# Neighbourhood attention stage: V asked for first in each unit, loads of K, Q and the bias tables dealt out one part to a unit

## The chip, the core and the metric

The kernel runs on one core of a Trainium2 chip. The core has a matrix engine (PE, with a separate row PEld for its weight loads), a vector engine (DVE), a scalar engine (ACT), a general engine (POOL) and a queue engine (SP) that only issues DMAs; 16 DMA engines move data between device memory (HBM) and the on-chip memory. Each engine runs its own instructions in their program order. The metric is device time in microseconds (us) of one execution, lower is better.

## The reference

One layer of a hybrid encoder, 1024 tokens of width 1024. After an RMS norm, one projection makes the inputs of two attention groups; their outputs are gated, joined and projected back, and a per-layer embedding is added. The change lies in group B alone, the neighbourhood attention: 8 heads of width 64 on a grid of 16 rows by 64 columns, where a query sees 8 rows by 16 columns of keys.

```python
s = jnp.einsum('bhrcd,bhrikd->bhrcik', qg, kg) * (d ** -0.5) + bias[None]
s = jnp.where(valid[:, None, :], s, NEG)
pr = jax.nn.softmax(s.reshape(B, H, R, GRID_W, kr * GRID_W), axis=-1)
o = jnp.einsum('bhrcik,bhrikd->bhrcd', pr, vg)
yb = neighbourhood_attention(qb, kb, vb, na_rpb[i]) * jax.nn.silu(zb)
```

## The kernel before, in words

All arithmetic is in float32, with operands split in a high and a low part where more precision is needed. The stages follow each other: norm and input projection (to about 304 us), neighbourhood attention (about 304 to 469 us) with the z projection mixed in as filling work, differential attention, output projection, gate.

The neighbourhood stage works through 32 units, numbered here 0 to 31: `(pr, R, j)` with 4 pairs of heads `pr`, 2 halves of the grid rows `R`, 4 column strips `j`. Four units with the same pair and half are called a block here, so a pair has two blocks. In iteration `i` of the loop the engines get, in this order: the loads of `pre(i + 1)`; the transposes `na_t` of unit i-1; the scores' bias and exponential `na_e` of unit i (DVE, ACT); filling matmuls; the gating `na_y` of unit i-2; the scores `na_s` of unit i+1 (PE, tile `nsp`, line 647); filling matmuls; the product with V, `na_pv`, of unit i-1 (PE, tile `npv`, line 700).

The loads come from HBM, where the projection stage had put Q, K and V:

- V: one tile `Vw` for each unit, in three DMAs of 64 or 48 KB, two on SP's queue and one on POOL's. `load_v` asks for it two units ahead of the unit whose loads `pre` handles.
- Q: for each block three parts of 256 KB (`Q1` upper and lower half from `qbh`, `Q2` from `qbl`). The scores of the block's first unit need all three.
- K: for each pair three parts of 512 KB (`kbh`, `kbl`, `kbh` again into `K2`).
- R: for each pair two bias tables of 376 KB, one for each head; `na_e` needs them from the pair's first unit on.
- `zraw`: 512 KB of weights for the z projection, asked for within the filling work, on the same SP queue.

There is no scheduler: the order of instructions on every engine is that of the code. SP's DMAs take eight semaphores in turn, and each issue waits, besides its buffer, for the one that had the same semaphore before, so that at most eight of SP's DMAs are under way.

Of the kernel before, what the change touches and what calls it, by code (L numbers as in the profile page):

```python
# [8 lines left out]
F32R = mybir.dt.float32r  # L9
# [6 lines left out]
P = 128  # L16
D = 1024
S = 1024
# [13 lines left out]
def ap_of(t, off, dims):  # L32
    return bass.AP(tensor=t.tensor, offset=t.offset + off, ap=[list(d) for d in dims])
# [7 lines left out]
def layer_kernel(ctx, tc, x, p, ngr, w_in, w_out, gains, lamv, t5p, rpbp, w_gate, w_ple,  # L41
# [9 lines left out]
    def nm(s):  # L51
        cnt[0] += 1
        return f"{s}_{cnt[0]}"

    def T8(shape, dt=F32, n="t8"):
        return sb.tile(shape, dt, name=nm(n), tag="b8", bufs=16)

    def T4(shape, dt=F32, n="t4"):
        return sb.tile(shape, dt, name=nm(n), tag="b4", bufs=8)

    def TA(shape, dt=F32, n="ta"):
        return sb.tile(shape, dt, name=nm(n), tag="a4", bufs=6)
# [4 lines left out]
    def T15(shape, dt=F32, n="t15"):  # L67
        return sb.tile(shape, dt, name=nm(n), tag="b2", bufs=NB2)
# [24 lines left out]
    def raw(a):  # L93
        return a.bitcast(F32) if a.dtype == F32R else a

    def ld(o, i):
        return nc.sync.dma_start(raw(o), raw(i))  # L97
# [504 lines left out]
    kb = {}  # L602
    qb = {}
    Rt = {}
    Vw = {}

    def load_k(pr):
        k1 = T8([P, 2, S], F32R, n="K1")
        h, l = qkd["kb"]
        for (dst, s) in ((k1[0:64], h), (k1[64:128], l), (K2[pr % 2][0:64], h)):  # L610
            ld(dst, s[pr].rearrange("(h d) s -> d h s", h=2))
        kb[pr] = k1

    def load_q(pr, R):
        q1 = T4([P, 2, 512], F32R, n="Q1")
        h, l = qkd["qb"]
        for (dst, s) in ((q1[0:64], h), (q1[64:128], h), (Q2[R][0:64], l)):
            ld(dst, s[pr, :, R * 512:(R + 1) * 512].rearrange("(h d) s -> d h s", h=2))
        qb[pr, R] = q1

    def load_r(pr):
        r = []
        for h in range(2):
            t = TA([P, 752], n="R")
            ld(t, ap_of(rpbp, (2 * pr + h) * 23 * 48 + 1, [[48, 8], [1, 16], [1, 752]]))
            r.append(t)
        Rt[pr] = r

    def load_v(pr, R, j):
        w = WID[j]  # L630
        v = T15([P, 3, P], n="Vw")
        for m in range(3):
            r0 = 4 * R + 4 * m
            (ld if m < 2 else stp)(v[0:4 * w, m], ap_of(vbd, (r0 * 64 + COL0[j]) * 512 + pr * P, [[64 * 512, 4], [512, w], [1, P]]))
        Vw[pr, R, j] = v
# [85 lines left out]
    K2 = []  # L721
    Q2 = []
# [109 lines left out]
    def pre(i):  # L832
        if i >= len(units):
            return
        pr, R, j = units[i]
        if j == 0:
            if R == 0:
                load_q(pr, 1)
            elif pr + 1 < 4:
                load_q(pr + 1, 0)  # L840
        if (R, j) == (0, 2) and pr + 1 < 4:
            load_k(pr + 1)
        if (R, j) == (1, 1) and pr + 1 < 4:
            load_r(pr + 1)
        if i + 2 < len(units):
            load_v(*units[i + 2])

    LA = 8
    load_p(1)
# [86 lines left out]
    def s7():  # L936
# [11 lines left out]
        30: lambda: u_load(30),  # L948
        31: lambda: u_load(31),
        NS - 7: lambda: (na_consts_k(), load_k(0)),  # L950
        NS - 5: lambda: (load_r0(), x_reload()),
        NS - 4: lambda: (z_load(COL["zb"], True), z_load(COL["zb"] + P, True)),
        NS - 2: lambda: (na_consts_q(), load_q(0, 0), load_v(0, 0, 0), load_v(0, 0, 1), z_split(COL["zb"], 0, 4),
                         z_split(COL["zb"], 4, 8), z_low()),
        NS - 1: lambda: (pre(0), x_resplit()),
        NS: na_consts_k,
    }
    lam_in = []
    normed = []
    for i in range(len(steps) + 2):  # L960
# [8 lines left out]
        if got:  # L969
            n, t0, c = got  # L970
# [314 lines left out]
    for i in range(NU + 3):  # L1285
        if i < NU:
            pre(i + 1)
# [171 lines left out]
```

## Time and profile before

| | |
|---|---|
| time, median of 3 runs | 822.54 us (818.36 to 823.64) |
| the profiled execution's own time | 819.77 us, its span 818.0 us |
| PE busy | 782.3 us, 96% of the span |
| DVE, ACT, POOL busy | 63%, 53%, 35% |
| DMA | 151.99 MB, mean 186 GB/s |

The span runs from the first to the last instruction; the device time has 1.8 us more. A busy share is an average over all stages, and PE counts as busy while its matmuls run at half clock too.

### The profile page before, as it was taken

To read this page: it belongs to the slowest core of one execution; us is meant where nothing else is said; L and a number is where in the kernel's file an instruction comes from. 1 tells how busy PE (TensorE), PEld (TensorE's weight loads), DVE (VectorE), ACT (ScalarE), POOL (GpSimd) and SP (SyncE) were. 2 spreads that over 40 slices of the span, in tenths; PEclk is the share of its full clock that TensorE was granted. 3 is DMA by queue.
4 is the path that set the end of the run, shared out by engine and by line. 5 is a ranking of instruction groups with operands and counts; after the bars stand their busy time and mean duration, and the time that the engine had idled before them with its cause. 6 is when DMAs were issued, how large, how long until landed. Compare 5 with 4: busy or idle time off the path is not lost.

```text
span 818.0 us, 12241 instructions
## 1 busy us (share of the span) xinstructions
PE 782.3 (96%) x4242; PEld 647.7 (79%) x4242; DVE 514.4 (63%) x990; ACT 437.4 (53%) x814; POOL 289.1 (35%) x303
## 2 busy tenths in 40 slices
PE   7999899999989999998989989999999989999997
PEld 6788688888878877776777767888888878888886
DVE  4758985786997675564645577777777652633332
ACT  5865454244545445554545588888898842311120
POOL 1001443261655421231323144777777643100000
PEclk9999899999999999999999999999999999999999
DMA  8855362853788999696967977578576518022322
GB/s 319 323 193 193 117 207 92 306 141 102 196 285 233 220 326 237 151 235 147 213 176 191 256 228 204 135 183 217 161 209 164 194 65 331 29 94 87 97 84 91
DMA packets 116622, 151.99 MB, mean 186 GB/s; under 512 B 25576, under 2 KB 74888, under 8 KB 116432
## 3 DMA queue, kind: packets, MB, share of 16 engines
q1 hardware_dynamic: 111824, 141.46, 59.5%
q0 software_dynamic: 4736, 9.75, 4.1%
q8 instruction: 34, 0.56, 0.3%
q14 instruction: 28, 0.23, 0.1%
HBM read 104.96 MB, written 46.17 MB: 185 GB/s over the span
## 4 chain that ended last, share of the span: by engine, by line
PE 67%; DMA 10%; DVE 9%; ACT 4%; SPq 4%; issue 3%; POOL 1%; DVEq 0%; POOLq 0%; ACTq 0%
PE ips L234 6%; PE ips L236 6%; PE ips L235 6%; PE dsp L1066 6%; DMA Vw<-vb 5%; PE gps L1259 4%; PE gps L1261 4%; PE gps L1260 4%; SPq L97 4%; PE dtp L1108 3%; PE ntp L685 2%; PE pps L314 2%; PE dpv L1135 2%; PE oap L1230 2%; PE npv L700 2%
## 5 line engine op out<-in xcount | busy, mean ns | idle before, releaser
L234 PE MATMUL ips<-w,xh 128*128 128x512 f32 x336 | 134.5, 400 | 3.7 <-DVE C L260 3.0
L236 PE MATMUL ips<-w,xl 128*128 128x512 f32 x336 | 132.1, 393 | 0.0
L235 PE MATMUL ips<-w,xh 128*128 128x512 f32 x336 | 131.8, 392 | 0.0
L1091 POOL TENSOR_TENSOR s<-s,s 128x1024 f32<-128x1024 f32 x32 | 77.1, 2410 | 56.1 <-ACT s L1090 54.4
L433 POOL TENSOR_TENSOR qrs<-qms,nhalf 128x16 f32<-128x16 f32 x16 | 51.4, 3215 | 91.6 <-DVE qms L431 91.6
L1076 DVE CUSTOM_DVE_ANT_0 s<-dsp,T 128x1024 f32<-128x1024 f32 x64 | 77.7, 1215 | 2.6 <-PE dsp L1066 2.6
L234 PEld LDWEIGHTS ips<-w,xh 128*128 128x128 f32 x336 | 63.8, 190 | 17.2 <-issue 3.8
L1078 ACT ACTIVATE s<-s,dm 128x1024 f32<-128x1024 f32 x64 | 73.3, 1146 | 4.6 <-DVE dm L1076 4.5
L236 PEld LDWEIGHTS ips<-w,xl 128*128 128x128 f32 x336 | 63.8, 190 | 13.9
L1066 PE MATMUL dsp<-K,Q 128*128 128x512 f32 x256 | 69.7, 394 | 4.9 <-DVE dm L1076 4.4
L1115 DVE TENSOR_TENSOR aTl<-dtp,aTh 128x512 fp32r<-128x512 f32 x64 | 44.3, 692 | 47.2 <-ACT aTh L1109 47.2
L235 PEld LDWEIGHTS ips<-w,xh 128*128 128x128 f32 x336 | 63.9, 190 | 12.7
L218 DVE TENSOR_TENSOR w<-wraw,w 128x512 fp32r<-128x512 f32 x84 | 62.2, 780 | 6.3 <-ACT w L217 6.0
L687 ACT ACTIVATE PT<-ntp 96x768 f32<-96x768 f32 (+1 forms) x32 | 25.9, 811 | 66.8 <-PE ntp L685 66.8
L716 POOL TENSOR_TENSOR yb<-nay,yb 128x128 fp32r<-128x128 f32 x32 | 18.1, 564 | 113.0 <-ACT yb L715 105.6
L1066 PEld LDWEIGHTS dsp<-K,Q 128*128 128x128 f32 x256 | 45.9, 189 | 14.7 <-issue 3.1
L582 PE MATMUL zps<-xh,zw 128*128 128x512 f32 x128 | 53.8, 420 | 0.0
L217 ACT ACTIVATE w<-wraw 128x512 fp32r<-128x512 f32 x84 | 48.5, 626 | 4.7 <-DVE wraw L193 4.5
L1263 ACT ACTIVATE gth<-gps 128x512 f32<-128x512 f32 x16 | 9.6, 597 | 77.2 <-PE gps L1261 72.4
L584 PE MATMUL zps<-xh,zw 128*128 128x512 f32 x128 | 50.6, 395 | 0.0
L583 PE MATMUL zps<-xl,zw 128*128 128x512 f32 x128 | 50.6, 395 | 0.0
L1259 PE MATMUL gps<-wgh,x1h 128*128 128x512 f32 x128 | 50.5, 395 | 0.0
(179 smaller groups left out, 1876.2 us busy)
## 6 DMA issues: line engine op xcount, KB each, us to landing
wraw<-in_w_in_dram SPq DMA_DIRECT2D x72, 256.0 KB
x<-in_x_dram SPq DMA_DIRECT2D x8, 512.0 KB
ppd<-pp SPq DMA_DIRECT2D x8, 512.0 KB
K<-kbh SPq DMA_DIRECT2D x8, 512.0 KB
Q<-qbh SPq DMA_DIRECT2D x16, 256.0 KB
Q<-qah SPq DMA_DIRECT2D x16, 256.0 KB
Q<-qal SPq DMA_DIRECT2D x16, 256.0 KB
wor<-in_w_out_dram SPq DMA_DIRECT2D x8, 512.0 KB
```

The lines of the kernel that those rows point to most:

```text
L218: V.tensor_tensor(w[:, 1], r, w.bitcast(F32)[:, 0], op=OP.subtract)
L234: mm(ps, lh[:, k, a:a + P], w[:, 0], start=(new and k == 0), stop=False, skip_group_check=cont)
L235: mm(ps, lh[:, k, a:a + P], w[:, 1], start=False, stop=False, skip_group_check=cont)
L236: mm(ps, ll[:, k, a:a + P], w[:, 0], start=False, stop=(k == 3), skip_group_check=cont)
L433: G.tensor_tensor(rs, ms, nhalf, op=OP.pow)
L582: mm(ps, w[:, 0, kc], xh(kc, a, b), start=(kc == 0), stop=False)
L583: mm(ps, w[:, 0, kc], xl(kc, a, b), start=False, stop=False)
L1066: mm(ps[:, cs], q[g][:, m, u * P:(u + 1) * P], k[:, cs], start=(g == 0), stop=(g == 1))
L1076: V.tensor_tensor_reduce(out=s, in0=ps, in1=back(Td[h][:, :], 1919 - (896 - P * qt), [[-1, S]]), scale=-1.0, scalar=BIG, op0=OP.add, op1=O ...
L1078: act(s, s, AF.Exp, bias=mx, scale=-1.0, accum_out=z[:, m:m + 1])
L1091: G.tensor_tensor(s1, s1, s2, op=OP.add)
L1259: mm(ps, h[:, k], wh, start=(k == 0), stop=False)
```

## The change

In `pre` the V of the unit two further on is asked for first, where it stood last. The three parts of Q, which were asked for together at a block's first unit (`j == 0`), are asked for at `j` = 0, 1 and 2, one at each. The three parts of K, together at `(R, j) = (0, 2)` before, come at (0, 2), (0, 3) and (1, 0). The two bias tables, together at (1, 1) before, come at (1, 1) and (1, 2). No DMA is added or left out, none changes its size or its queue.

```diff
-    def load_k(pr):
-        k1 = T8([P, 2, S], F32R, n="K1")
+    def load_k(pr, parts=(0, 1, 2)):
+        if 0 in parts:
+            kb[pr] = T8([P, 2, S], F32R, n="K1")
+        k1 = kb[pr]
         h, l = qkd["kb"]
-        for (dst, s) in ((k1[0:64], h), (k1[64:128], l), (K2[pr % 2][0:64], h)):
-            ld(dst, s[pr].rearrange("(h d) s -> d h s", h=2))
-        kb[pr] = k1
+        for i, (dst, s) in enumerate(((k1[0:64], h), (k1[64:128], l), (K2[pr % 2][0:64], h))):
+            if i in parts:
+                ld(dst, s[pr].rearrange("(h d) s -> d h s", h=2))
...
-        if j == 0:
-            if R == 0:
-                load_q(pr, 1)
-            elif pr + 1 < 4:
-                load_q(pr + 1, 0)
-        if (R, j) == (0, 2) and pr + 1 < 4:
-            load_k(pr + 1)
-        if (R, j) == (1, 1) and pr + 1 < 4:
-            load_r(pr + 1)
         if i + 2 < len(units):
             load_v(*units[i + 2])
+        if j < 3:
+            if R == 0:
+                load_q(pr, 1, (j,))
+            elif pr + 1 < 4:
+                load_q(pr + 1, 0, (j,))
+        if pr + 1 < 4:
+            if (R, j) in ((0, 2), (0, 3), (1, 0)):
+                load_k(pr + 1, (4 * R + j - 2,))
+            if (R, j) in ((1, 1), (1, 2)):
+                load_r(pr + 1, j - 1)
```

`load_q` and `load_r` are cut into parts in the same way as `load_k`.

On SP's queue, from the K of pair 1 to the V of unit 9. Before (each `Vw` row is the two DMAs of one unit, from unit 4 on; `Q_596` and `Q_537` are the three parts for the first block of pair 1, `K_572` and `K_551` the K of pair 1):

```order
L97 DMA K_572_2879<-kbh_107 64x2x1024
L97 DMA K_572_2879<-kbl_108 64x2x1024
L97 DMA K_551_2792<-kbh_107 64x2x1024
L97 DMA Vw_2883<-vb_111 96x1x128 x2
L97 DMA Vw_2929<-vb_111 128x1x128 x2
L97 DMA zraw_2954<-in_w_in_dram 128x8x128
L97 DMA Q_596_2985<-qbh_105 64x2x512 x2
L97 DMA Q_537_2707<-qbl_106 64x2x512
L97 DMA Vw_2989<-vb_111 128x1x128 x2
L97 DMA R_3041<-in_rpb_dram 128x1x752
L97 DMA R_3043<-in_rpb_dram 128x1x752
L97 DMA Vw_3045<-vb_111 96x1x128 x2
```

The same stretch of SP's queue now, from the V of unit 5 to the second bias table (`Q_597` and `Q_537` are the three parts of Q):

```order
L97 DMA Vw_2927<-vb_111 128x1x128 x2
L97 DMA K_573_2883<-kbl_108 64x2x1024
L97 DMA zraw_2953<-in_w_in_dram 128x8x128
L97 DMA Vw_2984<-vb_111 128x1x128 x2
L97 DMA Q_597_2988<-qbh_105 64x2x512
L97 DMA K_551_2790<-kbh_107 64x2x1024
L97 DMA Vw_3039<-vb_111 96x1x128 x2
L97 DMA Q_597_2988<-qbh_105 64x2x512
L97 DMA R_3044<-in_rpb_dram 128x1x752
L97 DMA Vw_3096<-vb_111 96x1x128 x2
L97 DMA Q_537_2707<-qbl_106 64x2x512
L97 DMA R_3101<-in_rpb_dram 128x1x752
```

The third part of Q (`Q_537`) stood ahead of the V of units 6, 7 and 8 and of both tables; now these three V and the first table stand ahead of it.

On SP's queue around the K of pair 2, before (`Vw_3263`, `Vw_3316` and `Vw_3378` are the V of units 11, 12 and 13):

```order
L97 DMA Vw_3263<-vb_111 96x1x128 x2
L97 DMA K_666_3312<-kbh_107 64x2x1024
L97 DMA K_666_3312<-kbl_108 64x2x1024
L97 DMA K_495_2460<-kbh_107 64x2x1024
L97 DMA Vw_3316<-vb_111 96x1x128 x2
L97 DMA Vw_3378<-vb_111 128x1x128 x2
```

And now (`Vw_3261`, `Vw_3311`, `Vw_3376`, `Vw_3428` are the V of units 11 to 14):

```order
L97 DMA Vw_3261<-vb_111 96x1x128 x2
L97 DMA Q_644_3210<-qbh_105 64x2x512
L97 DMA Vw_3311<-vb_111 96x1x128 x2
L97 DMA Q_538_2710<-qbl_106 64x2x512
L97 DMA K_667_3316<-kbh_107 64x2x1024
L97 DMA Vw_3376<-vb_111 128x1x128 x2
L97 DMA K_667_3316<-kbl_108 64x2x1024
L97 DMA Vw_3428<-vb_111 128x1x128 x2
```

The V of unit 12 stood behind three parts of K and stands ahead of all of them now, and two parts of Q have come between.

## Rows read from the trace of the kernel before

**Rows 1.** The page, part 4: the chain that ended last, by engine.

```profile
PE 67%; DMA 10%; DVE 9%; ACT 4%; SPq 4%; issue 3%; POOL 1%; DVEq 0%; POOLq 0%; ACTq 0%
```

**Rows 2.** Waits, 295 to 475 us: who waited for whom, total us, times, longest.

```profile
PE npv L700 <- DMA Vw<-vb: 5.1, 4, 1.9
PEld npv L700 <- DMA Vw<-vb: 4.2, 3, 2.1
```

**Rows 3.** Timeline of PE: start, us, instruction, count, idle time before and who ended it.

```profile
331.11 0.88 PE L647 MATMUL nsp<-K,Q 128*128 128x384 f32 x4
...
335.53 0.68 PE L647 MATMUL nsp<-K,Q 128*128 128x288 f32 x4
...
339.75 0.69 PE L647 MATMUL nsp<-K,Q 128*128 128x288 f32 x4
...
346.16 0.98 PE L647 MATMUL nsp<-K,Q 128*128 128x384 f32 x4 [1.36 <-DVE nam L662]
...
369.53 0.88 PE L647 MATMUL nsp<-K,Q 128*128 128x384 f32 x4
...
372.69 0.44 PE L700 MATMUL npv<-PT,Vw 96*64 96x128 f32 x4 [0.91 <-DMA Vw<-vb]
374.61 0.95 PE L700 MATMUL npv<-PT,Vw 96*64 96x128 f32 x8 [1.48 <-DMA Vw<-vb]
...
378.87 0.69 PE L647 MATMUL nsp<-K,Q 128*128 128x288 f32 x4
...
410.68 0.88 PE L647 MATMUL nsp<-K,Q 128*128 128x384 f32 x4
...
419.51 0.69 PE L647 MATMUL nsp<-K,Q 128*128 128x288 f32 x4
...
424.40 0.69 PE L647 MATMUL nsp<-K,Q 128*128 128x288 f32 x4
...
443.34 0.69 PE L647 MATMUL nsp<-K,Q 128*128 128x288 f32 x4
```

**Rows 4.** Chain of work, 290 to 420 us: start, us, what; a DMA from issue to landing.

```profile
328.48 8.75 DMA Q<-qbh
...
342.31 7.37 DMA Vw<-vb
...
359.46 15.10 DMA Vw<-vb
...
400.46 15.56 DMA Vw<-vb
```

**Rows 5.** Timeline of SP's queue: start, us, DMAs issued, count.

```profile
331.08 0.57 SPq L97 DMA_DIRECT2D Q<-qbl  x1
...
332.92 1.88 SPq L97 DMA_DIRECT2D R<-in_rpb_dram  x2
336.21 9.25 SPq L97 DMA_DIRECT2D Vw<-vb  x6
...
358.66 8.43 SPq L97 DMA_DIRECT2D Vw<-vb  x4
...
412.67 0.57 SPq L97 DMA_DIRECT2D Q<-qbl  x1
...
418.00 5.63 SPq L97 DMA_DIRECT2D Vw<-vb  x4
...
431.30 9.49 SPq L97 DMA_DIRECT2D Vw<-vb  x8
```

**Rows 6.** Timeline of DVE: scores plus bias, with the wait for the second table.

```profile
345.64 0.46 DVE L662 CUSTOM_DVE_ANT_1 nas<-nsp,R 128x288 f32<-128x288 f32 x1 [1.66 <-DMA R<-in_rpb_dram]
...
427.56 0.46 DVE L662 CUSTOM_DVE_ANT_1 nas<-nsp,R 128x288 f32<-128x288 f32 x1 [0.95 <-DMA R<-in_rpb_dram]
```

**Rows 7.** Windows: stretch, its us, busy PE, PEld, DVE, ACT, POOL, PEclk, DMA share, GB/s.

```profile
341.00:343.00 2.00, 2.00 (x20) 1.43 (x19) 1.12 (x3) 0.35 (x3) 1.12 (x2) 1.00 0.26 89
...
375.00:379.00 4.00, 4.00 (x19) 3.25 (x16) 0.00 (x0) 1.87 (x5) 0.00 (x0) 0.59 0.46 127
```

**Rows 8.** The tile Vw: its DMAs on SP, issue time in ns, shortest, median, longest.

```profile
L97 SPq DMA_DIRECT2D Vw<-vb x64: 516/659/7583, 298.4 to 455.6; - x64
```

More of the change, by code (lines that the diff above doesn't have):

```diff
@@ L605, in layer_kernel, with load_q, load_r @@
     Vw = {}
-    def load_k(pr):
-        k1 = T8([P, 2, S], F32R, n="K1")
+    def load_k(pr, parts=(0, 1, 2)):
+        if 0 in parts:
+            kb[pr] = T8([P, 2, S], F32R, n="K1")
+        k1 = kb[pr]
         h, l = qkd["kb"]
-        for (dst, s) in ((k1[0:64], h), (k1[64:128], l), (K2[pr % 2][0:64], h)):
-            ld(dst, s[pr].rearrange("(h d) s -> d h s", h=2))
-        kb[pr] = k1
-    def load_q(pr, R):
-        q1 = T4([P, 2, 512], F32R, n="Q1")
-        h, l = qkd["qb"]
[L617 to L627, printed above, removed]
+        for i, (dst, s) in enumerate(((k1[0:64], h), (k1[64:128], l), (K2[pr % 2][0:64], h))):
+            if i in parts:
+                ld(dst, s[pr].rearrange("(h d) s -> d h s", h=2))
+    def load_q(pr, R, parts=(0, 1, 2)):
+        if 0 in parts:
+            qb[pr, R] = T4([P, 2, 512], F32R, n="Q1")
+        q1 = qb[pr, R]
+        h, l = qkd["qb"]
+        for i, (dst, s) in enumerate(((q1[0:64], h), (q1[64:128], h), (Q2[R][0:64], l))):
+            if i in parts:
+                ld(dst, s[pr, :, R * 512:(R + 1) * 512].rearrange("(h d) s -> d h s", h=2))
+    def load_r(pr, h):
+        t = TA([P, 752], n="R")
+        ld(t, ap_of(rpbp, (2 * pr + h) * 23 * 48 + 1, [[48, 8], [1, 16], [1, 752]]))
+        Rt.setdefault(pr, []).append(t)
     def load_v(pr, R, j):
```

## The prediction

> **What bounds the kernel now.** I read the page first: the chain of work that ended last is PE for 67% and DMA for 10% [rows 1], so transfers do set part of the time. The list of waits says which in this stage: PE and its weight loads wait 9.3 us for V, in only 7 places [rows 2]. The timeline of PE then shows where: at the product of unit 12 (372.69 and 374.61, idle 0.91 and 1.48 us), and unit 20 in the same way. To price such a stall, idle time is not enough. An undisturbed step from one unit's scores to the next of this strip takes 4.42 us (331.11 to 335.53); the step with the stall takes 9.34 (369.53 to 378.87), and that of unit 20 takes 8.83 (410.68 to 419.51) [rows 3]. [...] A third stall is that of the bias tables: DVE waits for the second table of pair 1 until 345.64 [rows 6], and PE loses 1.36 us before unit 9's scores [rows 3]. Together 4.9 + 4.4 + 1.4 = 10.7 us, 1.3% of the time. More than that no order of these loads can win here.
>
> Why V is late: the load of unit 12's V that PE waited for took 15.10 us from its issue to its landing, that of unit 20 took 15.56, against 7.37 for a V load elsewhere [rows 4]. Both stand just behind three parts of K, 1.5 MB; at the page's mean rate of 186 GB/s these take 8 us, which is the difference.
>
> What matters most for the forecast is that the queue is never short of work. A V load of 64 KB takes 7.37 us to land, a part of Q 8.75 [rows 4], although an issue costs 0.66 us [rows 8]: what goes in stands behind some eight others. And SP itself is held up: six V loads take 9.25 us to issue, eight take 9.49 [rows 5], where 0.66 each would make 4.0 and 5.3. I read this as one line of transfers that is served in its order, with SP waiting at its end for landings. Such a line delivers the same total by the same time in any order; what a new order gives to one load it takes from another. In 341 to 343 us the mean share of the DMA engines is 0.26 [rows 7], while tables and V are under way and SP is held up, so a few engines must carry these loads. [...]
>
> **The change part by part.** Nothing is added or removed: the same DMAs, the same sizes, and on PE, DVE, ACT and POOL the same order (V's third part keeps its place on POOL, since only V is asked for there). Issue costs on SP stay, so this term is 0.
>
> *V first, K in three pieces.* The V of unit 12 and of unit 20 moves ahead of all three parts of K. It then lands some 8 us sooner than at 374.6, ahead of its product even if PE had not been held up before. Gain: 4.9 + 4.4 = 9.3 us, if nothing else is late. K itself has room: its last part is asked for two units before the third part of Q that the same scores need.
>
> *Q in three pieces.* The scores of a block's first unit need all three. Before, they were issued together, the third at 331.08, ahead of the scores at 339.75 of unit 8, which did not wait [rows 3, 5]. Now the third part stands behind the V of units 6, 7 and 8 and the first table. To see when it lands, I compare it with the second table, whose landing DVE shows: 345.64 [rows 6]. What stood ahead of that table then stands ahead of the third Q now, plus four V loads (units 7 and 8), minus that table itself. Four V loads are 4 x 0.66 = 2.6 us [rows 8], or 4 x 1.5 = 6.2 by the held-up row of 9.25 us for six [rows 5]; a table of 376 KB at 186 GB/s is 2.0 us. So the third Q lands at 345.6 - 2.0 + 2.6 = 346.2, by the other price at 349.8, and PE waits from 339.75: 6.5 us, at most 10. I take the lower, since SP's held-up time is spent behind the tables. This is a new wait where there was none.
>
> *The bias tables.* The second table now lands behind the third Q, at about 346.2 + 2.0 = 348.2. DVE wants it 4.2 us after the start of the scores (345.64 - 1.66 - 339.75), which is now 346.2 + 4.2 = 350.4. So the old wait of 1.4 us goes, but only because PE is later.
>
> *The sum.* In one line of transfers, waits do not add up: whoever waits lets the line get ahead, and the last late load sets the loss. So I ask at each place how far PE is behind a run without any wait. Before, it ends 10.7 us behind. For the first block of pair 3 the scores start at 424.40 [rows 3], so without waits at 413.7. The second table landed at 427.5 [rows 6]; the third Q again has four V loads more ahead of it (units 23 and 24) and that table not: 427.5 - 2.0 + 2.6 = 428.1, by the row of those very loads (5.63 us for four, rows 5) 431.1. That is 14.4 us behind, up to 17.4. For the second block of pair 3, three quarters of the row of eight V loads stand ahead (431.30 + 0.75 x 9.49 = 438.4 [rows 5]), landing 7.37 later at 445.8; the scores were at 443.34 [rows 3], without waits 432.6: 13.2 behind. The larger decides: 14.4 against 10.7, so +3.7 us, with bounds +2.5 (the second block alone) and +6.7. Clock lost behind the earlier new waits is inside this, since the next block start has to wait for its Q anyhow.
>
> Against the profiled execution this gives 819.8 + 3.7 = 823.5; the median of the three runs is 2.8 us above that execution, so the forecast is 822.5 + 3.7, about **826 us**, 0.4% slower: the waits for V turn into waits for Q. About 1% (8.2 us) is what a measurement of this kernel can tell from no change.
>
> **The rivals.**
>
> *As it reads:* V, K and Q all land in time, and the stalls go. For it: K is 8 us of queue in one piece before, and no longer; the third Q is issued two units ahead, 8.8 us of PE time. Against it: a part of Q takes 8.75 us to land even where it stands early [rows 4], which leaves nothing. It decides if the line has slack that I don't see, for example if big and small loads overlap better when mixed. Gain 9.3 to 10.7: 812 to 813 us.
>
> *No change in the total:* the few engines that the low share points to carry the same bytes by the same time, and the block starts end where they ended: the new order only changes the name of the load that is late. Then 822.5 us. [...] The same time comes out if the change doesn't do what it says, that is, if V, now asked for first, is held by a buffer that is still in use; against that, the long issues in rows 5 come behind large loads and not behind a late reader.
>
> *Slower by the sum:* the waits do add up, because the line does not get ahead while PE waits. That happens if V's buffers, which PE and POOL free unit by unit, become what SP waits for: V now stands first, so Q and K behind it wait with it. Then the starts of pairs 1, 2 and 3 pay 6.5, 3.7 and 3.7 us (the last is 428.1 - 424.4; pair 2 taken like pair 3), each with 2.5 us of low clock as behind unit 12 (4.9 - 2.4): 21.4 us, less the 10.7 that go: +10.7, or 833 us. It decides from the point where SP's issue of V waits for a reader and not for a landing.
>
> **How the numbers follow.** Forecast 826 (825 to 829): 0.45. No change in the total, 822.5: 0.20. Slower by the sum, 833: 0.21. As it reads, 812 to 813: 0.14. The limits of 1% lie at 814.3 and 830.8. Faster by over 1%: most of the last case, 0.12. Slower by over 1%: the third case and a little of the forecast's upper end, 0.23. Within: 0.65. The range of 8 in 10 reaches from 813, which leaves out half of the good case, to 834, which leaves out the upper part of the bad one.
>
> **What the profile of the changed kernel would show.** PE's waits for V at units 12 and 20 are gone. Instead the scores of a block's first unit wait for Q from `qbl`, first at about 339.75, for some 6 us, and less at later blocks; the step from unit 14 to 15 takes 4.4 us. DVE's wait for the second table is gone or short. A V load behind K no longer takes 15 us to land; the third part of Q still takes 6 to 9. If no scores wait for Q, the first rival is right and my line of transfers is wrong; if SP is seen waiting for readers of V's buffers, the third is. If Q is late by far less than 6 us at unit 8, the price of the V loads ahead of it is what I got wrong.

## The result, and the profile after

The changed kernel takes 830.55 us (median of 6 executions, 828.38 to 834.74), against 823.09 us for the kernel before in the same comparison: a ratio of 1.0111, 95% interval 1.0085 to 1.0136. By this ratio the change costs 9.1 us on 822.5, just over the 1% that a measurement can tell; the two medians lie 7.5 us apart. The profiled execution took 832.04 us, its span 830.3; the profiled pair therefore lies 12.3 us apart, a little more than the medians. One of e11's ten executions below (1098.1 us, granted clock 0.654) is left out of its median as slow.

The page of the changed kernel, part 4, gives the chain by engine, which answers to [rows 1]. PE and DMA are nearly where they were, and "issue", time for which the profile finds no releaser, has grown from 3% to 8%.

```profile
PE 66%; DVE 10%; DMA 9%; issue 8%; ACT 3%; POOL 3%; SPq 1%; POOLq 0%; DVEq 0%; ACTq 0%
```

The waits of the changed kernel, 295 to 490 us (who waited for whom, total us, times, longest), which answer to [rows 2]:

```profile
PE nsp L648 <- DMA Q<-qbl: 9.8, 4, 4.0
...
PEld nsp L648 <- DMA Q<-qbl: 7.2, 2, 4.3
...
PE nsp L648 <- issue: 5.2, 1, 5.2
...
DVE nas L663 <- DMA R<-in_rpb_dram: 2.0, 3, 1.4
```

PE no longer waits for V at all. It waits for the third part of Q instead, and for longer. The timeline of PE shows the places; the first row of each group is the first of a block's scores, which needs only the first two parts of Q, the second row the rest, with the idle time ahead of it, the third the next unit's scores:

```profile
321.43 0.29 PE L648 MATMUL nsp<-K,Q 128*128 128x288 f32 x1
...
324.37 0.64 PE L648 MATMUL nsp<-K,Q 128*128 128x288 f32 x3 [2.65 <-DMA Q<-qbl]
...
330.50 0.99 PE L648 MATMUL nsp<-K,Q 128*128 128x384 f32 x4 [0.26 <-ACT PT L688]
...
344.36 0.29 PE L648 MATMUL nsp<-K,Q 128*128 128x288 f32 x1
...
349.89 1.06 PE L648 MATMUL nsp<-K,Q 128*128 128x288 f32 x3 [5.24 <-issue]
...
357.35 0.87 PE L648 MATMUL nsp<-K,Q 128*128 128x384 f32 x4
...
391.45 0.29 PE L648 MATMUL nsp<-K,Q 128*128 128x288 f32 x1
...
394.27 0.66 PE L648 MATMUL nsp<-K,Q 128*128 128x288 f32 x3 [2.53 <-DMA Q<-qbl]
...
398.45 0.88 PE L648 MATMUL nsp<-K,Q 128*128 128x384 f32 x4
...
431.21 0.29 PE L648 MATMUL nsp<-K,Q 128*128 128x288 f32 x1
...
435.49 1.09 PE L648 MATMUL nsp<-K,Q 128*128 128x288 f32 x3 [3.99 <-DMA Q<-qbl]
...
442.16 0.87 PE L648 MATMUL nsp<-K,Q 128*128 128x384 f32 x4
```

These are the starts of units 4, 8, 16 and 24. The row at 349.89 names "issue" in place of a releaser; I read it as the same wait for the third Q, whose landing SP's semaphores put at 349.8. The steps from these units to the next take 9.1, 13.0, 7.0 and 11.0 us. The same steps without a wait take 4.6, 4.9, 4.2 and 4.2 (the second from the experiments e5 and e7 below, the others from the kernel before). So the four starts lose 4.5 + 8.1 + 2.8 + 6.8 = 22.2 us, on 14.4 us of idle time. The difference is the clock. Windows of the changed kernel (stretch, its us, busy PE, PEld, DVE, ACT, POOL, PEclk, DMA share, GB/s):

```profile
345.00:350.00 5.00, 0.11 (x1) 0.14 (x1) 1.01 (x3) 0.96 (x5) 1.26 (x2) 0.89 0.35 97
349.00:353.00 4.00, 3.11 (x9) 2.54 (x9) 0.93 (x4) 0.00 (x0) 0.00 (x0) 0.50 0.36 94
...
394.00:398.00 4.00, 3.73 (x29) 2.98 (x30) 1.13 (x5) 0.00 (x0) 0.51 (x1) 1.00 0.44 117
...
435.00:439.00 4.00, 3.52 (x18) 2.70 (x18) 0.93 (x4) 1.06 (x2) 0.00 (x0) 0.50 0.30 86
```

In the four microseconds behind the waits at units 8 and 24 the granted clock was 0.50, the lower of the two values that the trace's clock records hold (0.50 and 1.00); after the 2.53 us at unit 16 it stayed at 1.00. (Behind the 2.65 us at unit 4 it was 0.72 over 324 to 330 us.) The first row holds a second fact: while PE does nothing but wait for Q, the DMA engines are busy for only 0.35 of the time.

SP's queue (start, us, DMAs issued, count) shows what Q waits behind, as [rows 5] did before:

```profile
333.28 0.63 SPq L97 DMA_DIRECT2D R<-in_rpb_dram  x1
334.27 2.37 SPq L97 DMA_DIRECT2D Vw<-vb  x2
337.17 1.84 SPq L97 DMA_DIRECT2D Q<-qbl  x1
339.76 0.62 SPq L97 DMA_DIRECT2D R<-in_rpb_dram  x1
```

The third Q is asked for at 337.17, 6.1 us later than before [rows 5], and is there at 349.8. DVE's wait for the second table, which was 1.66 us [rows 6], is 0.28 in the timeline of DVE, since PE is late now:

```profile
351.74 0.46 DVE L663 CUSTOM_DVE_ANT_1 nas<-nsp,R 128x288 f32<-128x288 f32 x1 [0.28 <-DMA R<-in_rpb_dram]
```

The chain of work has these DMAs (start, us from issue to landing), which answer to [rows 4]; no V load of 15 us is left:

```profile
337.50 8.64 DMA Vw<-vb
...
385.09 9.14 DMA Q<-qbl
...
424.24 11.20 DMA Q<-qbl
```

### The profile page after: what moved, and what is told of

It reads as the page before. It is cut to its first block, busy times and chain, and to the rows that moved or that the text cites. A ratio compares the mean times of both kernels' runs of the same rounds, so it can differ in the third digit from the quotient of the medians.

```text
span 830.3 us, 12226 instructions
## 1 busy us (share of the span) xinstructions
PE 784.4 (94%) x4242; PEld 648.1 (78%) x4242; DVE 514.6 (62%) x990; ACT 437.4 (53%) x814; POOL 289.0 (35%) x303
## 4 chain that ended last, share of the span: by engine, by line
PE 66%; DVE 10%; DMA 9%; issue 8%; ACT 3%; POOL 3%; SPq 1%; POOLq 0%; DVEq 0%; ACTq 0%
PE dsp L1068 6%; PE ips L234 6%; PE ips L236 5%; PE ips L235 5%; PE gps L1261 4%; PE gps L1263 4%; PE gps L1262 4%; PE dtp L1110 3%; DMA Q<-qbl 2%; PE npv L701 2%; PE ntp L686 2%; PE zps L582 2%; PE zps L584 2%; PE zps L583 2%; PE dpv L1137 2%
## 5 line engine op out<-in xcount | busy, mean ns | idle before, releaser
L235 PEld LDWEIGHTS ips<-w,xh 128*128 128x128 f32 x336 | 63.6, 189 | 12.6
L582 PE MATMUL zps<-xh,zw 128*128 128x512 f32 x128 | 54.5, 426 | 0.0
L584 PE MATMUL zps<-xh,zw 128*128 128x512 f32 x128 | 51.6, 403 | 0.0
L1111 ACT ACTIVATE aTh<-dtp 128x512 fp32r<-128x512 f32 x64 | 38.0, 594 | 23.7 <-PE dtp L1110 23.7
```

The costliest lines, as they stand in the source:

```text
L235: mm(ps, lh[:, k, a:a + P], w[:, 1], start=False, stop=False, skip_group_check=cont)
L582: mm(ps, w[:, 0, kc], xh(kc, a, b), start=(kc == 0), stop=False)
L584: mm(ps, w[:, 1, kc], xh(kc, a, b), start=False, stop=(kc == 7))
```

## The experiments

Two measures stand beside the time of every run, both from its one profiled execution. The **stage** is the time from the first scores (`nsp`) to the end of the last product with V (`npv`) on PE's timeline. The **turn** is the time on SP's queue from the issue of the first part of K for pair 1 to that for pair 3. In between SP issues two pairs' worth of the same loads and four `zraw` (three in e8), without V's in e7, e9 and e10, so that the turn tells how fast the line takes them. SP's waits for buffers are in it too. In the turns of e7, e9 and e10 SP is ahead of PE and waits 30 to 38 us for products with V, so these three say nothing of the line. The list of SP's waits goes by closeness in time, and names readers in the middle of long issues too. SP's waits for landings of 0.25 us and more all end within 0.05 us of the issue that follows. By this mark SP waits for readers of its buffers 6 to 11 us in the turns of the kernels with V in strips (e5, e6, e11, e12), not at all in those of before, e1, e2, e3, e4 and e8, and twice in that of the changed kernel, for products with V. The changed kernel's list of SP's waits, 359 to 365 us:

```profile
SPq L97 <- PE npv L701: 3.2, 2, 2.6
```

Those two waits are behind the late start of unit 8.

| kernel | median us | ratio to before (95%) | stage us | turn us |
|---|---|---|---|---|
| before | 821.1 to 823.1 | 1 | 164.3 | 79.5 |
| after | 830.55 | 1.0111 (1.0085 to 1.0136) | 177.9 | 85.6 |
| e1 Q dealt out only | 829.22 | 1.0097 (1.0068 to 1.0127) | 171.6 | 81.1 |
| e2 K dealt out only | 824.50 | 1.0038 (1.0010 to 1.0067) | 173.3 | 84.4 |
| e3 V first only | 825.45 | 1.0042 (1.0018 to 1.0067) | 171.2 | 81.4 |
| e4 after, Q together | 831.67 | 1.0138 (1.0085 to 1.0192) | 171.3 | 84.8 |
| e5 V in strips | 819.23 | 0.9974 (0.9952 to 0.9996) | 155.4 | 68.6 |
| e6 after, V in strips | 823.84 | 1.0024 (0.9996 to 1.0052) | 159.3 | 73.7 |
| e7 V on POOL | 819.13 | 0.9965 (0.9943 to 0.9987) | 157.2 | 74.3 |
| e8 V first, K and R sooner | 828.96 | 1.0091 (1.0060 to 1.0122) | 172.9 | 79.8 |
| e9 V on POOL, not the first | 822.01 | 1.0012 (0.9987 to 1.0036) | 166.6 | 77.8 |
| e10 after, V on POOL | 825.85 | 1.0063 (1.0037 to 1.0088) | 170.0 | 79.1 |
| e11 strips copied by POOL | 816.83 | 0.9944 (0.9917 to 0.9971) | 154.6 | 68.2 |
| e12 strips stored at once | 818.93 | 0.9970 (0.9952 to 0.9987) | 155.9 | 68.5 |

One profiled execution can lie some microseconds off its median (e2's is 829.5 us, e1's 826.4), so stages are compared where they differ by more than that.

### One part of the change at a time: e1 to e4

The two theories were: A, the late third part of Q alone decides; B, every part that is dealt out or moved costs by itself, because the line is served worse.

e1 takes from the change only the parts of Q:

```diff
-        if j == 0:
+        if j < 3:
             if R == 0:
-                load_q(pr, 1)
+                load_q(pr, 1, (j,))
             elif pr + 1 < 4:
-                load_q(pr + 1, 0)
+                load_q(pr + 1, 0, (j,))
```

> The kernel before with one part of the change: the three parts of Q dealt out to three units; V asked for last, K and R together as before. Theory A (the third part of Q comes too late, and that alone decides): the waits for Q at the block starts are there in full, beside the old waits for V behind K: 829 to 836 us. Theory B (the line of transfers itself is slowed by mixing small loads between large ones, or by V standing first): little changes, 821 to 826 us.

e2 takes only the parts of K, e3 only the place of V, e4 takes all but the parts of Q, which are asked for together behind V:

```diff
-        if (R, j) == (0, 2) and pr + 1 < 4:
-            load_k(pr + 1)
+        if pr + 1 < 4 and (R, j) in ((0, 2), (0, 3), (1, 0)):
+            load_k(pr + 1, (4 * R + j - 2,))
```

> The kernel before with one part of the change: the three parts of K dealt out to three units; Q, R and V as before. Theory A: the waits for V at units 12 and 20 (9.3 us) shrink or go, nothing else is late: 812 to 819 us. Theory B: the mixing slows the line by some us, which shows as later landings; 821 to 826 us.

```diff
         pr, R, j = units[i]
+        if i + 2 < len(units):
+            load_v(*units[i + 2])
         if j == 0:
...
-        if i + 2 < len(units):
-            load_v(*units[i + 2])
```

> The kernel before with one part of the change: V asked for first in each unit; Q, K and R together as before. Theory A: V of unit 12 passes three parts of K, Q is put back by two V loads only (1.3 to 3 us, against a slack of 1 us at unit 8 and some 3 to 5 at others): 814 to 822 us. Theory B (V first makes Q and K wait for readers of V's buffers): 826 to 832 us.

```diff
         if i + 2 < len(units):
             load_v(*units[i + 2])
-        if j < 3:
+        if j == 0:
             if R == 0:
-                load_q(pr, 1, (j,))
+                load_q(pr, 1)
             elif pr + 1 < 4:
-                load_q(pr + 1, 0, (j,))
+                load_q(pr + 1, 0)
```

> The changed kernel with the three parts of Q asked for together again at the block's first unit, behind V. Theory A: V, Q and K in time, the bias table perhaps 1 to 3 us late: 813 to 820 us. Theory B: still slower than before, 825 to 830 us.

All four are slower than before, and each for another late load. The waits of e1:

```profile
PE nsp L648 <- DMA Q<-qbl: 7.4, 4, 3.7
```

The waits of e2, then of e3, then of e4:

```profile
DVE nas L663 <- DMA R<-in_rpb_dram: 18.1, 6, 5.7
...
PE nsp L648 <- DMA K<-kbh: 3.4, 2, 2.9
```

```profile
DVE nas L663 <- DMA R<-in_rpb_dram: 16.6, 6, 5.3
```

```profile
DVE nas L663 <- DMA R<-in_rpb_dram: 17.5, 5, 6.1
...
PE nsp L648 <- DMA K<-kbh: 2.8, 1, 2.8
```

With Q dealt out, the third Q is late; with Q together but V first or K dealt out, the bias tables are, and the last K. e1's 829.22 us lies in the range of theory A, e2's 824.50 in that of B, e3's 825.45 between the two ranges and e4's 831.67 above both. The parts do not add: the parts of Q alone cost as much as the whole change, within the intervals (1.0097 and 1.0111). Theory A as the whole account falls by e4: it puts Q back and stays at 1.0138. The wait for V had gone or shrunk in all four, and in each whatever stands last ahead of a pair's start had taken its place. Theory B fits for K, by a small margin: where K is dealt out (e2, e4, after) the turn is 84.4 to 85.6 us, without SP's two waits for V's products 82.4 in the changed kernel, and where K stays together (before, e1, e3) 79.5 to 81.4. Each turn is of one execution, and that of e2 was the slowest of its ten.

e8 is e3 with K asked for one unit and the tables two units sooner:

```diff
-        if (R, j) == (0, 2) and pr + 1 < 4:
+        if (R, j) == (0, 1) and pr + 1 < 4:
             load_k(pr + 1)
-        if (R, j) == (1, 1) and pr + 1 < 4:
+        if (R, j) == (0, 3) and pr + 1 < 4:
```

> Before with V first, as in the earlier run e3, and K asked for one unit sooner and both tables two units sooner. If the line is never short of work (as the prediction has it), asking sooner only moves the lateness: the start of pairs 1 to 3 gets K and R in time, but Q or V behind them is late by as much; 822 to 827 us. If the waits at the starts of the pairs came from asking too late, they go, V is in time too: 813 to 816 us.

It is slower still, above both expectations. K and tables are in time, and the scores of unit 8 wait for the Q behind them, as PE's timeline of e8 shows:

```profile
348.93 1.72 PE L648 MATMUL nsp<-K,Q 128*128 128x288 f32 x4 [9.57 <-issue]
```

So the lateness can be handed from load to load, and none of these orders removes it.

### V laid out by strips: e5, e6, e11, e12

V's source in HBM is 4 groups of 24 or 32 rows, one group for a grid row. e5 lays V out once by column strips, so that a load reads 96 or 128 rows that follow each other; the order of the loads is that of before:

```diff
+    vbs = [DT([16, WID[j], 512], n="vbs") for j in range(4)]
...
+    def v_strips():
+        for j in range(4):
+            ld(vbs[j], ap_of(vbd, COL0[j] * 512, [[64 * 512, 16], [512, WID[j]], [1, 512]]))
...
-            (ld if m < 2 else stp)(v[0:4 * w, m], ap_of(vbd, (r0 * 64 + COL0[j]) * 512 + pr * P, [[64 * 512, 4], [512, w], [1, P]]))
+            (ld if m < 2 else stp)(v[0:4 * w, m], ap_of(vbs[j], r0 * w * 512 + pr * P, [[512, 4 * w], [1, P]]))
...
+        27: v_strips,
```

> The order of the loads is that of before; only V's source changes: four copies within HBM during the projection stage (3.7 MB more) lay V out by column strips, so that one V load reads 96 or 128 rows that follow each other, in place of 4 groups of 24 or 32 rows. Theory C (few DMA engines carry a V load, and their backlog is what makes V, R and Q late): a V load then spreads over all engines, the idle time of PE for V at units 12 and 20 (5.1 us before, 9.3 us of lengthened steps) goes, and the second table lands earlier: 9 us less in the stage, 813 to 815 us. Theory D (the line is limited by bytes, or by SP and its eight semaphores, not by a few engines): the waits at units 12 and 20 stay at 4 to 6 us, time within 3 us of before, or up to 5 us more for the copies.

e6 is the same edit in the changed kernel.

> The changed kernel with the same copies by strips. Theory C: the waits for Q at units 4, 8, 16 and 24 (some 14 us of idle time in the changed kernel) shrink to under 4 us together, 813 to 817 us, so that the order hardly matters any more. Theory D: the four waits stay, 828 to 833 us, as the changed kernel without the copies.

In e5 every wait of a matmul for V, Q, K or R inside the stage is gone; its list of waits has 0.8 us for Q at the stage's first scores, 0.7 us of weight loads for V, and no other matmul of PE waits for a DMA. The stage shrinks by 8.9 us, which is what the waits before had cost, and the turn from 79.5 to 68.6. The windows of before, and of e5 at the stretch that answers to it (the stage starts 8.2 us later there):

```profile
337.00:347.00 10.00, 8.64 (x63) 6.67 (x62) 4.66 (x17) 4.79 (x13) 1.96 (x4) 1.00 0.43 125
```

```profile
345.00:355.00 10.00, 10.00 (x73) 7.85 (x73) 5.77 (x21) 4.79 (x14) 2.90 (x6) 1.00 0.85 215
```

The DMA share is 0.85 where it was 0.43, the rate 215 GB/s where it was 125. The trace has one sign more: the semaphore of a load rises in steps until the load has landed. In before all 64 of SP's V loads have 5 steps, the bias tables 9, the parts of Q and K 16. In e5, e6, e11 and e12 V has 16 as well, and the others are as before. The packets go with the steps: in the stage of before at most 4 packets of SP's V loads move at once for 94% of the time that any of them moves (`zraw`'s loads left out), at most 8 of the tables' for 97%, but 12 or more of Q's and K's for 53%. So I read fewer steps as fewer engines on a load, which is an inference: no run names the engines. Theory C is right about the stage: with the same bytes in the same order on the same queue, V's waits and those behind it go when V is laid out by strips. The total missed theory C's 813 to 815 us, for a reason ahead of the stage (below). In e6 the waits at units 4, 16 and 24 are gone too, but one is left, on PE's timeline of e6, which theory C allowed (under 4 us) and e5 has not:

```profile
347.98 0.29 PE L653 MATMUL nsp<-K,Q 128*128 128x288 f32 x1
...
350.77 1.06 PE L653 MATMUL nsp<-K,Q 128*128 128x288 f32 x3 [2.50 <-issue]
```

The dealt-out order thus still loses 4 us of stage against e5, and its turn is 5.1 us longer. Its 823.84 us lie between the ranges of the two theories.

The time of e5 fell by only 0.3%, because the stage starts 8.2 us later. While the copies run, PE waits 4.5 us for a split weight tile (`w`), and its clock falls behind that wait, as the windows of e5 show:

```profile
232.00:238.00 6.00, 5.26 (x16) 4.19 (x17) 5.97 (x10) 2.19 (x4) 3.74 (x3) 0.55 0.98 281
```

e11 sends the copies over POOL's queue, e12 has no copies and writes the strips from the projection's own stores:

```diff
+            stp(vbs[j], ap_of(vbd, COL0[j] * 512, [[64 * 512, 16], [512, WID[j]], [1, 512]]))
```

> As e5 (V laid out by strips, order of before), but the four copies go over POOL's queue, so that no weight load of the projection stands behind them on SP's. If the 8 us that e5 lost ahead of the neighbourhood stage came from the place in SP's queue, the stage starts at 305 to 307 us and the time is 810 to 813 us; if it came from the bytes of the copies, it stays at 312 to 313 us and the time at 818 to 820 us.

```diff
-            pst.append(lambda: st(vbd[t0 * P:(t0 + 2) * P, :].rearrange("(u q) d -> q u d", q=P), c))
+            pst.append(lambda: v_strips(t0, c))
...
+    def v_strips(t0, c):
+        for j in range(4):
+            w = WID[j]
+            for rr in range(2):
+                p0 = rr * 64 + COL0[j]
+                st(ap_of(vbs[j], (2 * t0 + rr) * w * 512, [[512, w], [2 * w * 512, 2], [1, 512]]), c[p0:p0 + w])
```

> V laid out by strips as in e5, order of before, without the copies: the projection stage's own stores of V (4 DMAs between 139 and 155 us) become 32 smaller ones that write the strips at once (1.5 MB more, no reads more). Theory C: the neighbourhood stage is as short as in e5 (155.4 us from the first scores to the last product with V, against 164.3), and the stage starts at 304.8 to 307 us, if SP's 28 issues more (some 15 us of SP at 0.5 us each) delay no weights that PE waits for: 810 to 814 us, 1.0 to 1.5% faster than before. If those issues hold up the weight loads behind them, PE loses up to 8 us near 150 us and the time is 817 to 820 us, as e5 and e11. Theory D is out either way if the stage is again 155 us long.

Both have the short stage again (154.6 and 155.9 us), so theory D is out; both pay ahead of it. e11's stage starts at 314.1 us, no sooner than e5's 312.9, so the copies' place in SP's queue is not what e5 lost by; that their traffic is, as the expectation had it, is left over and not shown by itself. In e12 PE waits for a tile `C` of the projection, behind the stores. PE's timeline of e12, and its windows there:

```profile
170.03 0.77 PE L234 MATMUL ips<-w,xh 128*128 128x512 f32 x1 [5.83 <-DVE C L260]
```

```profile
164.00:170.00 6.00, 0.20 (x1) 0.00 (x1) 1.23 (x1) 0.09 (x1) 0.00 (x0) 0.86 0.87 296
170.00:176.00 6.00, 5.97 (x16) 4.76 (x17) 4.38 (x7) 3.67 (x7) 3.27 (x1) 0.57 0.05 18
```

SP's queue in e12 shows why DVE is late there: sixteen of the stores stand ahead of the two loads of `C` that DVE adds, which the kernel before asked for at 155.25.

```profile
155.29 8.57 SPq L100 DMA_DIRECT2D vbs<-C  x16
163.91 0.83 SPq L97 DMA_DIRECT2D C<-ud  x2
```

One wait of 5.8 us, and a clock of 0.57 behind it, costs nearly all that the strips give: e12's 818.93 us lie in the second of its ranges. e11 is the fastest kernel here, 0.6% faster than before and, by the ratios, 1.7% faster than the changed one.

The turns can be read from SP's queue, here in before, the first parts of K for pairs 1, 2 and 3, and the same rows of e12:

```profile
315.81 1.44 SPq L97 DMA_DIRECT2D K<-kbh  x1
...
354.85 0.62 SPq L97 DMA_DIRECT2D K<-kbh  x1
...
395.27 2.27 SPq L97 DMA_DIRECT2D K<-kbh  x1
```

```profile
321.26 0.59 SPq L97 DMA_DIRECT2D K<-kbh  x1
...
353.26 0.59 SPq L97 DMA_DIRECT2D K<-kbh  x1
...
389.71 0.58 SPq L97 DMA_DIRECT2D K<-kbh  x1
```

And in the changed kernel:

```profile
317.28 0.61 SPq L97 DMA_DIRECT2D K<-kbh  x1
...
358.34 0.61 SPq L97 DMA_DIRECT2D K<-kbh  x1
...
402.86 0.63 SPq L97 DMA_DIRECT2D K<-kbh  x1
```

The tile `Vw` in e12 (SP's issue time of a V load in ns, shortest, median, longest), against 516/659/7583 in [rows 8]:

```profile
L97 SPq DMA_DIRECT2D Vw<-vbs x64: 303/428/1841, 306.2 to 440.0; - x64
```

### V off SP's queue: e7, e9, e10

e7 sends all of V over POOL's queue, in the order of before; e9 leaves the V of units 0 to 2 on SP; e10 is e9's edit in the changed kernel.

```diff
-            (ld if m < 2 else stp)(v[0:4 * w, m], ap_of(...))
+            stp(v[0:4 * w, m], ap_of(...))
```

> Before, but all three DMAs of a V on POOL's queue, so that V stands behind no K, Q or R on SP's queue. If the place in SP's queue and SP's hold-ups make V late, the waits at units 12 and 20 go, and K, Q and R, with nothing between them, come no later than before: 812 to 815 us, if POOL issues in time. If the DMA engines themselves are the line, V waits there for the same K packets: V at units 12 and 20 stays late by 3 to 5 us each, 820 to 825 us. If POOL is held up by the issues (64 more), its filling work comes late and PE waits for POOL or DVE: over 825 us.

```diff
+            (ld if m < 2 and (pr, R, j) < (0, 0, 3) else stp)(v[0:4 * w, m], ap_of(...))
```

> The order of before; V on POOL's queue from unit 3 on, the V of units 0 to 2 as before on SP's. Theory C (what makes a load late is that V shares SP's queue and its few engines with K, Q and R): the wait of 3.9 us for Q at the stage's start, seen with all of V on POOL, goes, nothing else is late, 810 to 814 us. Theory D (POOL's DMAs at the stage's start were not what made that Q late): the start stays at 309 us, 817 to 820 us.

> The changed kernel's order of K, Q and R with V on POOL's queue in the same way. Theory C: without V in SP's queue the parts dealt out have nothing small between them; the waits for Q at units 4, 8, 16, 24 go or stay under 3 us in all, within 3 us of e9. If dealing out the parts itself makes them late (asked for one or two units later), the wait at unit 8 stays above 2 us and the time is 4 to 8 us above e9.

e7 loses nothing from unit 1 on, but its first scores wait 3.9 us for Q, ahead of the stage's 157.2 us. It beats before by 0.35%; its 819.13 us lie between its first two ranges. e9 takes off more than half of that wait (1.5 us are left) and was to gain by it, but has a new one, for the second table at unit 9, on PE's timeline of e9:

```profile
356.04 1.65 PE L647 MATMUL nsp<-K,Q 128*128 128x384 f32 x4 [5.70 <-DVE nam L662]
```

e9's expectation is missed, and why the table comes some 9 us later than in e7 (355.5 against 346.8, by SP's semaphores) is open: the loads differ by six V loads alone. Of the 9 us, 4.1 are there when SP issues the table (330.70 against 326.59). e10 waits 5.05 us for the third Q at unit 8, as after does, and is 3.8 us slower than e9. The second half of e10's expectation holds, the time at its edge: dealing Q out makes it late at unit 8 even where no V of SP's stands between its parts.

## Why the prediction was right, and where it was not

The forecast was 826 us, range 813 to 834; the result is 830.55 us. Sign and range are right, and what takes the place of what is right too: V's waits turn into waits for Q. The size is off: +3.7 us forecast, +9.1 by the ratio and +7.5 by the medians measured. The sum's own bounds end at 829; the range held because it took in part of a rival, which is luck for the forecast itself.

- *V's waits at units 12 and 20 go.* They do. Their price, 4.9 and 4.4 us (9.34 and 8.83 less 4.42), was too high. The working takes 4.42 us for an undisturbed step, which is the step of unit 6; in e5 the two stalled steps take 5.1 and 4.8 us. So the stalls cost 4.2 and 4.0 us, and the stage of e5, without any wait, is 8.9 us shorter than that of before, against the 10.7 of the working. Nor do the 9.3 us of waits in 7 places bear it out: they add waits of PE and of its weight loads that overlap. PE's own idle time for V is 5.1 us in 4 places [rows 2].
- *The third Q lands at 346.2, or 349.8 by the held-up price, and the lower is taken.* It landed at 349.8. The choice between the two prices failed: SP's held-up time is not "spent behind the tables", since V ahead of Q holds SP up as well (2.37 us for two loads in the rows above, in place of 1.3). From issue to landing this part took 12.6 us and those of pairs 2 and 3 took 9.1 and 11.2, where 6 to 9 were foreseen.
- *Unit 4.* The working looks at the starts of pairs 1 and 3 and not at the first block that the change reaches. The third Q of unit 4 is asked for two units later as well and costs 4.5 us.
- *One line delivers the same total by the same time in any order, so waits do not add up.* This is the step that failed most. By it PE would be 14.4 us behind at unit 24, or 17.4 by the higher price; it is 22.2 behind, each of the four starts having added its own wait. The last late load does set the loss, but it landed at 435.4 in place of the 428.1 of the sum, 7.3 us later. The line did not get ahead: the same loads took 85.6 us in place of 79.5, and 3.2 of these 6.1 us are SP's two waits for products with V, behind the late start of unit 8. With the parts of Q alone (e1) the turn stays at 81.1 us, and the stage is 16.2 us longer than that of e5, where that of the changed kernel is 22.5 longer.
- *Clock lost behind the new waits is inside the sum.* It adds up with the waits: 22.2 us on 14.4 of idle time. Beyond their idle time the four starts lost 1.9, 2.9, 0.3 and 2.8 us; the 2.5 us at every start, in the sum of 833, was an estimate from unit 12 alone.
- *The rivals.* "Slower by the sum", 833, described the outcome better than the forecast did: the waits do add up. But its mechanism, SP held by readers of V's buffers, is seen ahead of the last late Q in two places only, for the 3.2 us above, and before has none there. Such waits alone make no load late: in e12 the list of SP's waits names `npv` for 36.9 us in 9 places (270 to 475 us), against 16.9 in 8 in the changed kernel, and no matmul of PE waits for a load behind the stage's first scores. "No change in the total" rested on the few engines, and the packets bear these out for V; that the order cannot matter did not follow, as e5 and e6 differ by 4 us too.
- *Few engines carry V.* The row it was inferred from does not show it: by the sizes of the packets, what moved between 341 and 343 us [rows 7] was nearly all of the bias tables (59 packets of a table's 3008 bytes, one of V's 512). The runs bear the inference out all the same: at most 4 of V's packets move at once for 94% of the time that any does in before, and V's semaphore rises in 5 steps there and in 16 in e5, e11 and e12, which change nothing else in the stage and in which no matmul waits for V any more. The DMA share over ten microseconds goes from 0.43 in before to 0.85 in e5.

What stays open: why dealing K out makes the turn longer in e2 and e4, by 3 to 5 us. That with small loads between K's parts fewer bytes are under way in SP's eight semaphores would fit, but nothing here measured it by itself. The few engines of V are not the whole of it: the turn of e6 is 5.1 us longer than that of e5, though SP waits for readers some 11 us in both. Open are also the late table of e9, and what exactly e11 loses ahead of the stage.

## What to carry to other kernels

Where loads of one queue are late, look first at the DMA share while they are waited for. Here it was 0.35 while PE stood still; V laid out so that a load reads rows that follow each other took the waits away (a share of 0.85 in e5, 0.43 in before), and each new order only chose which load is late. Let the late load be one whose wait is cheap; here a start that needs all of Q at once was the dearest place, with up to 8.1 us lost against 4.2 and 4.0 at the products that waited for V, and with Q dealt out its third part was asked for 6.1 us later. A store or copy that prepares a better layout has its own price: here it cost nearly all that the layout gave (8.2 of 8.9 us in e5), and the matrix engine waited behind it (4.5 us in e5, 5.8 in e12). And price a stall against the same step without it, not against a step that looks like it.

## What the runs showed of the hardware

- A wait of PE costs more than its length, but not always: behind 5.24 and 3.99 us of idle time the clock was 0.50, behind 0.91 and 1.48 us close together 0.59 [rows 3, 7], behind 2.53 us alone at unit 16 it stayed 1.00 and that start lost only 2.8 us. The 2.65 us at unit 4, hardly longer, cost 4.5.
- The semaphore of one of SP's loads rises in 5 steps for V from 4 groups of rows, in 9 for a table from 8 groups, in 16 for Q, K and V by strips. In before at most 4 of V's packets move at once for 94% of the time that any does, at most 8 of the tables' for 97%, and 12 or more of Q's and K's for 53%.
- Laying V out by rows that follow each other also shortened SP's issue of a load, from a median of 659 ns to 428, besides the hold-ups (7.6 us longest to 1.8).
- The same loads in the same order on one queue need 79.5 us or 68.5, by V's source alone, although V's loads on SP's queue are a small part of what stands there: 16 units of two loads of 64 or 48 KB, 1.8 MB, beside 7.8 MB of K, Q and R for the two pairs.
